# FFN operands emitted chunk by chunk, convolution columns loaded one mixer sooner, and a probability tile's two parts read bank by bank

## The chip, the cores and the metric

The kernel runs on one core of one Trainium2 chip. The metric is the device time of one execution in microseconds (us), as a median over several runs. The core has a matrix engine (PE in the profile, its weight loads PEld), a vector engine (DVE), a scalar engine (ACT), GpSimd (POOL) and the SyncE queue that starts transfers (SP, shown as SPq).

## The reference, cut to what matters

Two network blocks run one after the other on 1,024 tokens of width 1,024, all in float32. Block one has a differential attention layer and a latent attention layer (MLA, 8 heads). Block two has a mixing layer, made of a gated spatial mixer, six stick-breaking heads and six dilated-window heads, and then a feed-forward layer (FFN) with a short convolution:

```python
def _mla(...):                                   # block one, second layer
    sc = (einsum('bqhd,bkhd->bhqk', qn, k_nope) + einsum('bqhr,bkr->bhqk', qp, k_pe)) * scale
    p = softmax(sc)
    return einsum('bhqk,bkhd->bqhd', p, v)       # p times v

def second_block(...):
    h = _rmsnorm_2(x, g_mix[l]) * (1.0 + scale1) + shift1
    a_u, a_v, b_q, b_k, b_v, c_q, c_k, c_v = split(h @ w_in[l])
    y = concat([spatial_gating(a_u, a_v), stick_breaking(b_q, b_k, b_v), dilated_window(c_q, c_k, c_v)])
    x = x + (1.0 + gate1) * (y @ w_out[l])
    h = _rmsnorm_2(x, g_ffn[l]) * (1.0 + scale2) + shift2
    up = causal_dwconv(h @ w_up[l], conv_w[l], conv_b[l])
    gate, val = split(up)
    x = x + (1.0 + gate2) * ((silu(gate) * val) @ w_down[l])
```

## The kernel before, in words

Every float32 operand of a product is held as two parts that PE reads at a faster rate: an upper part `hi` (a cast, by ACT) and a lower part `lo = x - hi` (a subtraction, mostly by DVE). A product is then three matmuls, or four where one factor is exact.

The program is one long Python function. A scheduler orders each engine's instructions by priority, which is the order in which the code emits them, lifted by `ahead(tc, generator, offset)` for attention work; so a change in the order of the code can move instructions on every engine. Tiles come from pools with a fixed number of buffers per tag (`h4`, `pt`, `e`, `t2`, `wr` and so on); a load into a tag whose buffers still come from an earlier stage is preceded by a one-column copy on GpSimd (`load`).

The stretches of the profiled execution are: differential attention 0 to 800 us; MLA projections to 1045, MLA heads to 1435; in the mixing layer the gated and the dilated mixers to about 1835 and three pairs of stick-breaking heads to about 2093; then the output projection, the FFN's normalisation (`next_h`) and the FFN (a Strassen product of 7 instead of 8 block products) to the end. Next to an attention's steps the projections of the next head or pair run as filler, paced by `merge` and `pace`; beside the last pair runs the first half of the output projection.

**pt_fill.** In MLA heads and in stick-breaking heads the probabilities of 128 queries (a row block, `slot`) are turned for the product with v. PE transposes up to four 128x128 tiles into one PSUM bank (`ps`, seen in the trace as `m<-cr,e`), ACT casts them in pairs to `hi` (`pt<-m`), DVE subtracts to `lo` (`pt<-m,pt`), and `pv` then multiplies (`m<-pt,v`). The framework keeps two engines from reading one PSUM bank at the same time: they take turns, each with a wait on the other.

**mixers.** The list of six attentions is 0 to 2 dilated, 3 to 5 stick-breaking pairs 0 to 2. After the loop over the first five, `columns` loads the convolution weights (`load_rows`: three small transfers from `in_conv_w_dram` into two `t2` tiles on SP's queue) and turns them (`turn_rows`: one PE transpose and one DVE copy each).

**next_h.** For each half of the tokens, 8 chunks of 128x512 are scaled (DVE, `scalar_tensor_tensor`), shifted (ACT, `Identity` with a bias), and those of half 0 are made into FFN operands by `operand` (a cast on ACT, a subtraction on DVE, `h<-ab,h`).

Of the kernel before, what the change touches and what calls it, by code (L numbers as in the profile page):

```python
# [44 lines left out]
def alternate(a, b):  # L45

    for _ in a:
        next(b, None)
        yield
    yield from b  # L50


def drain(g):
    for _ in g:
        pass


def ahead(tc, gen, offset):

    if not offset:  # L60
        yield from gen
        return
    while True:
        with tc.high_priority(offset):
            x = next(gen, drain)
        if x is drain:
            return
        yield x


def some(g, n):

    for _ in range(n):
        if next(g, drain) is drain:
            return
        yield


def merge(main, fill, lead=0):

    for _ in range(lead):
        next(fill, None)
    for _ in main:
        next(fill, None)
    drain(fill)


def pace(main, total, early, fill, n):

    w = done = 0  # L90
    for x in main:
        w += x or 1
        if next(early, 0) == 0:
            while done < n * w / total:
                next(fill, None)
                done += 1
    drain(early)
    drain(fill)
# [24 lines left out]
class Net:  # L123
# [446 lines left out]
    def next_h(self, proj, xbox, acc, acol, shift):  # L570


        nc = self.nc
        hs, ops, phase = [], {}, self.phase
        for half in range(2):
            self.phase = phase
            drain(proj[half])
            self.phase = phase + 1
            xt, rr = xbox[half][1], self.stat_end(acc[:, half], D)
            for c in range(8):  # L580
                nc.vector.scalar_tensor_tensor(xt[c], xt[c], acol[:, c:c + 1], rr, ALU.mult, ALU.mult)
                nc.scalar.activation(xt[c], xt[c], AF.Identity, bias=shift[:, c:c + 1])
            hs.append(xt)
            if half == 0:
                for i, c in ((1, 0), (2, 4)):
                    ops[i] = [self.operand(x) for x in xt[c:c + 4]]
        return hs, ops

    def turn_ops(self, ops, b11, b12, b21, b22):
# [223 lines left out]
    def pt_fill(self, pts, p, slot, ktiles):  # L813

        nc = self.nc
        qs = slice(slot * 128, slot * 128 + 128)
        for g in range((ktiles + 3) // 4):
            n = min(4, ktiles - 4 * g)
            ps = self.pm((128, 4, 128))
            for i in range(n):  # L820
                kt = 4 * g + i
                nc.tensor.transpose(ps[:, i], p[:, kt * 128:(kt + 1) * 128], self.ident)
            for i in range(0, n, 2):
                m = min(2, n - i)
                hi, lo = (pts[4 * g + i + x][:, 0:m, qs] for x in range(2))
                nc.scalar.copy(hi, ps[:, i:i + m])
                self.lo(lo, ps[:, i:i + m], hi)

    def pv(self, v, pts):

# [1103 lines left out]
    def mixers(self, hts):  # L1934
        nc, a = self.nc, self.a
        w = a["w_in_2"][0]
        od = self.scratch([8, 128, S], "od2")
        self.od2 = od
        lse, fac = self.scratch([2, 6, S], "lse"), self.scratch([6, S], "fac")
        dil = (1, 4, 16)  # L1940

        def qk(i, box):
            return self.mixer_c_qk(w, i, dil[i], hts, box) if i < 3 else self.mixer_b_qk(w, i - 3, hts, box)

        vcol = lambda i: 2432 + i * 128 if i < 3 else 1280 + (i - 3) * 128
        self.off_b = self.mask_tile("off_b", ALU.is_gt, [[-1, 128]], 1)
        ma = self.mixer_a(w, hts, od)
        def qkv(i, box, vbox):
            yield from qk(i, box)
            yield from self.mixer_v(w, vcol(i), hts, dil[i] if i < 3 else 1, vbox)  # L1950

        box, vbox = [], []
        next(ma)
        next(ma)
        drain(alternate(qkv(0, box, vbox), some(ma, 4)))
        for i in range(5):
            cur, cv, box, vbox = box, vbox, [], []
            nxt = qkv(i + 1, box, vbox)
            if i < 3:
                att = self.mixer_c_attention(i, dil[i], *cur, cv, lse, od)  # L1960
                merge(ahead(self.tc, att, HP_C), alternate(ma, nxt) if i == 0 else nxt, LEAD_C)
            else:
                att = self.mixer_b_attention(i - 3, *cur, cv, od)
                pace(ahead(self.tc, att, HP_B), 72, iter(()), nxt, 8)
            if i == 2:
                self.alphas_c(lse, fac)
        self.columns("cols_a", 88, ["conv_w0", "conv_w1"])
        self.columns("cols_b", 56, ["conv_w2"])
        m2 = self.mod
        acol = self.scale_col(self.col["g_ffn_2"], m2["scale_f"], "acol3")  # L1970
        self.xs3 = self.scratch([D, S], "xs3")
        ots = [[None] * 8, [None] * 8]
        acc = self.t("z", [128, 2, 512])
        self.sign = acc[:, 0, 0:1]
        xbox = [[], []]
        proj = [
            self.out_proj(a["w_out_2"][0], ots[half], m2["gate_m"], self.xs2, self.xs3, half, tags, [None],
                          [acc[:, half]], xbox[half])
            for half, tags in enumerate((("kk", "kk", "ab", "ab"), ("pt",) * 4))]
        cs = ((0, 1), (2, 3), (5, 6), (7,))  # L1980
        self.last_head(
            self.mixer_b_attention(2, *box, vbox, od, ots), 20, 52, iter(()),
            [self.load_o(od, half, cs, ots[half], fac) for half in range(2)], proj[0])
        return self.next_h(proj, xbox, acc, acol, m2["shift_f"])
# [176 lines left out]
```

## Time and profile before

| | before |
|---|---|
| median of 3 runs | 2925.15 us (2916.08 to 2933.80) |
| the profiled execution | 2909.92 us, of which the span is 2907.9 us |
| PE busy, of the span | 2629.5 us, 90% |
| DVE busy | 2099.3 us, 72% |
| ACT busy | 1421.6 us, 49% |
| POOL busy | 1292.2 us, 44% |

The span runs from the first to the last recorded instruction; 2.0 us lie around it. An engine's busy time says how much of the span it worked; idle time is put down to what ended it. A wait of PE counts for most here, since PE is nearest to full.

### The profile page before, as it was taken

What the parts mean: (1) busy time and instruction counts of PE and PEld (TensorE: products, weight loads), DVE (VectorE), ACT (ScalarE), POOL (GpSimd) and SP (SyncE); (2) the same over time, 40 slices, a digit from 0 to 9 for tenths busy, and PEclk for the clock granted to TensorE, in tenths of its full rate; (3) what the DMA queues carried; (4) which work ended last, traced back from release to release, by engine and by line L of the source; (5) the groups of instructions that cost most, each with busy time, mean ns of one, the idle gap of its engine ahead of it and who ended that gap; (6) DMA issues with size and microseconds to landing.
All of it is one profiled execution on the core that took longest, in us unless ns stands there. A gap on an engine that the chain in (4) does not pass through costs nothing. (4 is left out here: it accounts for less than half of the span.)

```text
span 2907.9 us, 34523 instructions
## 1 busy us (share of the span) xinstructions
PE 2629.5 (90%) x12023; PEld 2128.7 (73%) x12023; DVE 2099.3 (72%) x2696; ACT 1421.6 (49%) x2609; POOL 1292.2 (44%) x779
## 2 busy tenths in 40 slices
PE   7899999998899979999997798887978999997897
PEld 4678787887777867877775687776766777776676
DVE  7577877778642596667768563778768888899865
ACT  5455555556444534544554453667544344443432
POOL 2423323342344532212243332444447878778761
PEclk8999999999999999999998999999989999998998
DMA  7233333234541473223342356332621222234564
GB/s 292 66 97 101 109 109 105 66 95 141 174 131 42 127 254 106 71 89 118 117 132 80 80 82 112 91 87 85 197 89 51 88 79 73 87 124 146 187 237 147
DMA packets 308402, 338.91 MB, mean 117 GB/s; under 512 B 37428, under 2 KB 232068, under 8 KB 308228
## 3 DMA queue, kind: packets, MB, share of 16 engines
q1 hardware_dynamic: 308228, 336.69, 39.3%
q8 instruction: 96, 1.57, 0.2%
q14 instruction: 78, 0.64, 0.1%
HBM read 231.17 MB, written 60.89 MB: 100 GB/s over the span
## 5 line engine op out<-in xcount | busy, mean ns | idle before, releaser
L111 PE MATMUL m<-h,wh 128*128 128x512 f32 x3480 | 985.0, 402 | 48.1 <-DVE h L111 14.4
L111 PEld LDWEIGHTS m<-h,wh 128*128 128x128 f32 x3480 | 669.4, 194 | 204.2 <-DVE h L111 18.2
L111 POOL TENSOR_TENSOR wl<-wr,wh 128x1024 fp32r<-128x1024 f32 (+1 forms) x146 | 333.5, 2291 | 429.6 <-ACT wh L111 393.4
L111 PE MATMUL u<-h,wh 128*128 128x512 f32 x1264 | 408.3, 404 | 1.4 <-ACT h L111 0.8
L111 POOL TENSOR_SCALAR e<-e,cf 128x1024 f32<-128x1024 f32 x128 | 152.6, 1193 | 564.8 <-DVE cf L111 403.5
L111 PE MATMUL m<-h,wl 128*128 128x512 f32 x840 | 336.8, 402 | 7.8 <-POOL wl L111 7.8
L111 ACT ACTIVATE e<-s,cf 128x1024 f32<-128x1024 f32 x192 | 216.0, 1126 | 240.4 <-DVE cf L111 221.9
L111 ACT CAST wh<-wr 128x1024 fp32r<-128x1024 f32 (+3 forms) x252 | 202.6, 810 | 170.1 <-PE m L111 67.7
L111 DVE TENSOR_REDUCE cf<-s 128x1 f32<-128x1024 f32 x192 | 228.3, 1217 | 69.6 <-PE s L111 69.2
L111 PEld LDWEIGHTS u<-h,wh 128*128 128x128 f32 x1264 | 233.1, 191 | 47.5 <-ACT h L111 1.2
L111 PE MATMUL u<-h,wl 128*128 128x512 f32 x632 | 252.5, 400 | 12.7 <-POOL wl L111 12.7
L111 PE MATMUL s<-kk,qq 128*128 128x512 f32 (+3 forms) x752 | 187.3, 386 | 35.8 <-DVE e L111 18.7
L111 ACT CAST pt<-m 128x256 fp32r<-128x256 f32 (+2 forms) x396 | 140.1, 376 | 155.1 <-PE m L111 88.4
L111 PE MATMUL s<-h,wh 128*128 128x512 f32 x720 | 182.8, 399 | 35.5 <-DVE h L111 18.2
L111 PEld LDWEIGHTS m<-h,wl 128*128 128x128 f32 x840 | 164.1, 195 | 44.5 <-POOL wl L111 9.0
L111 DVE SCALAR_TENSOR_TENSOR e<-z,cf,e 128x1023 f32<-128x1023 f32 (+1 forms) x88 | 175.8, 2008 | 24.8 <-ACT e L111 24.6
L111 PE MATMUL s<-h,h 128*128 128x512 f32 x640 | 171.5, 414 | 20.8 <-DVE h L111 14.3
L111 PEld LDWEIGHTS s<-h,wh 128*128 128x128 f32 x720 | 136.5, 192 | 71.3 <-DVE h L111 19.7
L111 DVE TENSOR_TENSOR pt<-m,pt 128x256 fp32r<-128x256 f32 (+2 forms) x396 | 155.0, 416 | 41.6 <-ACT pt L111 34.6
L111 PEld LDWEIGHTS s<-kk,qq 128*128 128x128 f32 x752 | 135.9, 196 | 65.8 <-DVE e L111 20.4
L111 PE MATMUL m<-pt,v 128*128 128x512 f32 (+3 forms) x668 | 151.9, 371 | 17.1 <-ACT pt L111 8.6
L111 PEld LDWEIGHTS s<-h,h 128*128 128x128 f32 x640 | 122.3, 196 | 52.5 <-DVE h L111 17.8
(285 smaller groups left out, 4848.0 us busy)
## 6 DMA issues: line engine op xcount, KB each, us to landing
wr<-in_w_in_dram SPq DMA_DIRECT2D x61, 512.0 KB
wr<-in_w_out_dram SPq DMA_DIRECT2D x48, 512.0 KB
tb<-in_w_ada_dram SPq DMA_DIRECT2D x48, 512.0 KB
wr<-in_w_up_dram SPq DMA_DIRECT2D x47, 512.0 KB
qq<-ab SPq DMA_DIRECT2D x144, 128.0 KB
wr<-in_ada_w_dram SPq DMA_DIRECT2D x32, 512.0 KB
tf<-act SPq DMA_DIRECT2D x30, 512.0 KB
wr<-in_w_down_dram SPq DMA_DIRECT2D x30, 512.0 KB
```

Of the source, the lines that this page charges most:

```text
L111: ins = f(*args, **kw)
```

## The change

Three edits. In `next_h` the operand of a chunk of half 0 is emitted straight after the chunk's scale and shift, and no longer after all eight chunks. In `pt_fill` all casts of a bank are emitted first and then all its subtractions, where before each cast was followed by its subtraction. In `mixers` the convolution weights are loaded into their two `t2` tiles ahead of stick-breaking pair 1 (`i == 4`); the transposes stay after the loop.

```diff
@@ next_h
             xt, rr = xbox[half][1], self.stat_end(acc[:, half], D)
+            for i in (1, 2):
+                ops.setdefault(i, [])
             for c in range(8):
                 nc.vector.scalar_tensor_tensor(xt[c], xt[c], acol[:, c:c + 1], rr, ALU.mult, ALU.mult)
                 nc.scalar.activation(xt[c], xt[c], AF.Identity, bias=shift[:, c:c + 1])
+                if half == 0:
+                    ops[1 + c // 4].append(self.operand(xt[c]))
             hs.append(xt)
-            if half == 0:
-                for i, c in ((1, 0), (2, 4)):
-                    ops[i] = [self.operand(x) for x in xt[c:c + 4]]
@@ pt_fill
                 nc.tensor.transpose(ps[:, i], p[:, kt * 128:(kt + 1) * 128], self.ident)
-            for i in range(0, n, 2):
-                m = min(2, n - i)
-                hi, lo = (pts[4 * g + i + x][:, 0:m, qs] for x in range(2))
-                nc.scalar.copy(hi, ps[:, i:i + m])
-                self.lo(lo, ps[:, i:i + m], hi)
+            parts = [(pts[4 * g + i], pts[4 * g + i + 1], i, min(2, n - i)) for i in range(0, n, 2)]
+            for hi, _, i, m in parts:
+                nc.scalar.copy(hi[:, 0:m, qs], ps[:, i:i + m])
+            for hi, lo, i, m in parts:
+                self.lo(lo[:, 0:m, qs], ps[:, i:i + m], hi[:, 0:m, qs])
@@ mixers, in the loop over i in range(5) and after it
             nxt = qkv(i + 1, box, vbox)
+            if i == 4:
+                rows = [self.load_rows(names) for names in (["conv_w0", "conv_w1"], ["conv_w2"])]
             ...
-        self.columns("cols_a", 88, ["conv_w0", "conv_w1"])
-        self.columns("cols_b", 56, ["conv_w2"])
+        for args, rws in zip((("cols_a", 88), ("cols_b", 56)), rows):
+            self.turn_rows(*args, *rws, self.pm((128, 128)))
```

DVE's order at the end of the first MLA head, where its last product with v goes into `t` and the next head's operand `h` is split; `pt` are subtractions of two banks (`m_9237` and `m_9246`), `z` is an accumulation of the next block's modulation:

```order
 L111 TENSOR_TENSOR t_1454_8947<-m_9185,t_1454_8947 128x512
+L111 TENSOR_TENSOR pt_9213<-m_9237,pt_9212 128x2x128
+L111 TENSOR_TENSOR pt_9215<-m_9237,pt_9214 128x2x128
 L111 SCALAR_TENSOR_TENSOR z_11384<-tb_11783,cf,z_11384 128x1024
-L111 TENSOR_TENSOR pt_9213<-m_9237,pt_9212 128x2x128
+L111 TENSOR_TENSOR pt_9217<-m_9246,pt_9216 128x2x128
+L111 TENSOR_TENSOR pt_9219<-m_9246,pt_9218 128x2x128
+L111 TENSOR_TENSOR h_1512_9267<-m_9268,h_1512_9267 128x512
 L111 SCALAR_TENSOR_TENSOR z_11384<-tb_11786,cf,z_11384 128x1024
-L111 TENSOR_TENSOR h_1512_9267<-m_9268,h_1512_9267 128x512
```

Four subtractions, a bank's two next to each other, now stand ahead of `h`, and one of the two accumulations now stands behind it.

DVE's order in stick-breaking pair 0, where its second half of the queries begins; `e` are the clamps (minima) of the scores of successive row blocks, `tb` is a scan, `t` the sum of a product with v. Before:

```order
 L111 SCALAR_TENSOR_TENSOR tb_15668<-cf,tb_15668 128x1024
 L111 TENSOR_TENSOR pt_15486<-m_15507,pt_15485 128x2x128
 L111 TENSOR_SCALAR e_15758<-s_15752 128x640
 L111 TENSOR_SCALAR e_15785<-s_15779 128x768
 L111 TENSOR_TENSOR t_2483_15194<-m_15471,t_2543_15480 64x512
 L111 TENSOR_TENSOR pt_15486<-m_15534,pt_15485 128x2x128
 L111 TENSOR_TENSOR pt_15488<-m_15507,pt_15487 128x2x128
 L111 TENSOR_TENSOR pt_15490<-m_15516,pt_15489 128x128
 L111 TENSOR_SCALAR e_15813<-s_15807 128x896
```

And of the change, the same place:

```order
 L111 TENSOR_TENSOR t_2483_15194<-m_15471,t_2543_15480 64x512
 L111 TENSOR_SCALAR e_15758<-s_15752 128x640
 L111 TENSOR_TENSOR pt_15486<-m_15507,pt_15485 128x2x128
 L111 TENSOR_TENSOR pt_15488<-m_15507,pt_15487 128x2x128
 L111 TENSOR_TENSOR pt_15490<-m_15516,pt_15489 128x128
 L111 TENSOR_TENSOR pt_15486<-m_15534,pt_15485 128x2x128
 L111 TENSOR_TENSOR pt_15488<-m_15534,pt_15487 128x2x128
 L111 TENSOR_SCALAR e_15785<-s_15779 128x768
 L111 SCALAR_TENSOR_TENSOR tb_15668<-cf,tb_15668 128x1024
 L111 TENSOR_SCALAR e_15813<-s_15807 128x896
```

The second clamp now stands behind five subtractions in a row, and the scan behind the first two clamps.

SP's queue, where the convolution weights are started; `wr` is a block of output weights, `od` an attention result that is written to memory. Before, at the end of pair 1:

```order
 L111 DMA wr_17198<-in_w_out_dram 128x8x128
-L111 DMA t_2755_16588<-in_conv_w_dram 44x128 x2
-L111 DMA t_2757_16595<-in_conv_w_dram 44x128
-L111 DMA od_13122<-t_2680_16181 128x512
```

And of the change, at the end of pair 0:

```order
 L111 DMA wr_16942<-in_w_out_dram 128x8x128
+L111 DMA t_2619_15891<-in_conv_w_dram 44x128 x2
+L111 DMA t_2620_15895<-in_conv_w_dram 44x128
 L111 DMA od_13122<-t_2544_15484 128x512
```

The three transfers are started one pair of heads sooner, again just ahead of the write of an attention result.

## Rows read from the trace of the kernel before

**Rows 1.** The page: span, and busy time, share of the span and number of instructions of each engine.

```profile
span 2907.9 us, 34523 instructions
PE 2629.5 (90%) x12023; PEld 2128.7 (73%) x12023; DVE 2099.3 (72%) x2696; ACT 1421.6 (49%) x2609; POOL 1292.2 (44%) x779
```

**Rows 2.** Busy time by stretch (MLA heads, stick-breaking pairs): us of the stretch, then busy us and number of instructions of PE, PEld, DVE, ACT and POOL, the granted clock as a share of full speed, the share of the DMA engines and GB/s.

```profile
1045.00:1435.00 390.00, 365.91 (x1843) 301.00 (x1842) 273.13 (x546) 193.53 (x450) 95.64 (x85) 0.97 0.37 114
1835.00:2093.00 258.00, 216.44 (x1061) 178.82 (x1062) 205.66 (x284) 164.87 (x328) 117.98 (x63) 0.93 0.36 102
```

**Rows 3.** The instructions on tile `pt`, MLA heads: engine, operation, count, shortest, median and longest in ns, first and last start, forms.

```profile
L111 ACT CAST pt<-m x234: 361/373/422, 1050.0 to 1431.0; 128x256 fp32r<-128x256 f32 x117
L111 DVE TENSOR_TENSOR pt<-m,pt x233: 398/416/426, 1055.0 to 1434.7; 128x256 fp32r<-128x256 f32 x117
```

**Rows 4.** Waits of all engines, MLA heads: who waited, for whom, us in total, times, longest.

```profile
ACT pt L111 <- DVE pt L111: 47.2, 55, 2.4
DVE pt L111 <- ACT pt L111: 22.6, 32, 3.0
```

**Rows 5.** Waits of PE alone, 1045 to 1400 us, same columns.

```profile
PE s L111 <- DVE h L111: 8.5, 3, 3.5
PE m L111 <- DVE pt L111: 1.3, 2, 0.8
```

**Rows 6.** Busy time in stretches of 10 us behind the start of three MLA heads, columns as in rows 2.

```profile
1140.00:1150.00 10.00, 10.00 (x48) 8.15 (x47) 8.21 (x16) 4.21 (x12) 0.73 (x1) 0.83 0.59 200
1240.00:1250.00 10.00, 9.37 (x38) 7.60 (x39) 7.23 (x15) 3.87 (x12) 0.73 (x1) 0.69 0.71 240
1340.00:1350.00 10.00, 7.43 (x26) 6.00 (x26) 8.18 (x13) 2.86 (x9) 0.43 (x1) 0.66 0.39 135
```

**Rows 7.** The timelines of DVE, ACT and PE around the start of an MLA head (1131 to 1142 us), and of PE at two later heads: start, us, engine, operation, tiles, count, and in brackets the idle time before it and what ended it.

```profile
1134.82 0.68 DVE L111 TENSOR_TENSOR t<-m,t 128x512 f32<-128x512 f32 x1
1135.49 1.28 DVE L111 SCALAR_TENSOR_TENSOR z<-tb,cf,z 128x1024 f32<-128x1024 f32 x1
1136.70 0.42 DVE L111 TENSOR_TENSOR pt<-m,pt 128x256 fp32r<-128x256 f32 x1
...
1138.54 0.69 DVE L111 TENSOR_TENSOR h<-m,h 128x512 fp32r<-128x512 f32 x1
...
1132.51 0.37 ACT L111 CAST pt<-m 128x256 fp32r<-128x256 f32 x1 [5.55 <-PE m L111]
...
1137.15 0.65 ACT L111 CAST pt<-m 128x256 fp32r<-128x256 f32 x2 [0.46 <-DVE pt L111]
...
1139.28 1.19 PE L111 MATMUL s<-h,h 128*128 128x512 f32 x4 [2.53 <-DVE h L111]
...
1240.63 2.08 PE L111 MATMUL s<-h,h 128*128 128x512 f32 x4 [2.54 <-DVE h L111]
...
1342.57 2.07 PE L111 MATMUL s<-h,h 128*128 128x512 f32 x4 [3.45 <-DVE h L111]
```

**Rows 8.** Waits of PE, stick-breaking pairs (1830 to 2093 us), columns as in rows 4.

```profile
PE s L111 <- DVE e L111: 18.7, 13, 6.4
PE m L111 <- DVE pt L111: 4.5, 6, 1.6
PE m L111 <- DMA t<-in_conv_w_dram: 2.2, 2, 2.1
PE m L111 <- ACT pt L111: 0.8, 2, 0.5
```

**Rows 9.** Waits of ACT and DVE for each other at `pt`, stick-breaking pairs (1835 to 2093 us), columns as in rows 4.

```profile
ACT pt L111 <- DVE pt L111: 7.1, 6, 2.1
DVE pt L111 <- ACT pt L111: 5.8, 10, 1.4
```

**Rows 10.** The timelines of DVE and of PE where the second half of stick-breaking pair 0 begins (1876 to 1888 us), columns as in rows 7.

```profile
1878.54 2.47 DVE L111 TENSOR_TENSOR_SCAN tb<-cf,tb 128x1024 f32<-128x1024 f32 x1 [0.26 <-ACT tb L111]
1880.93 0.39 DVE L111 TENSOR_TENSOR pt<-m,pt 128x256 fp32r<-128x256 f32 x1
1881.24 1.67 DVE L111 TENSOR_SCALAR e<-s 128x640 f32<-128x640 f32 x2
...
1883.67 0.95 DVE L111 TENSOR_TENSOR pt<-m,pt 128x256 fp32r<-128x256 f32 x3
...
1882.11 1.86 PE L111 MATMUL s<-kk,qq 128*128 128x512 f32 x4 [3.05 <-DVE e L111]
```

**Rows 11.** The timelines of PE, SP and POOL at the turning of the convolution weights (1999 to 2007 us), columns as in rows 7.

```profile
2005.41 0.27 PE L111 MATMUL m<-cr,t 88*128 88x88 f32 x1 [2.06 <-DMA t<-in_conv_w_dram]
...
2003.44 1.11 SPq L111 DMA_DIRECT2D t<-in_conv_w_dram  x3
...
2003.23 0.30 POOL L111 COPY t<-z 128x1 f32<-128x1 f32 x2
```

**Rows 12.** The last subtraction of an FFN operand of half 0 on DVE, and PE at the start of the FFN (2118 to 2152 us), columns as in rows 7.

```profile
2122.73 0.68 DVE L111 TENSOR_TENSOR h<-ab,h 128x512 fp32r<-128x512 f32 x1
...
2151.59 0.63 PE L111 MATMUL m<-h,wh 128*128 128x512 f32 x1
```

**Rows 13.** Groups of DVE instructions, stick-breaking pairs: count, busy us, mean ns of one, idle time before.

```profile
L111 DVE TENSOR_TENSOR h<-tf,h 128x512 fp32r<-128x512 f32 x14 | 12.9, 956 | 0.8 <-ACT h L111 0.7
L111 DVE TENSOR_TENSOR z<-z,tf 128x512 f32<-128x512 f32 x7 | 12.3, 1760 | 1.0 <-ACT tf L111 0.7
```

## The prediction

> **What bounds the kernel now.** I read the page first: PE is busy 2629.5 of 2907.9 us, DVE 72%, and nothing else is above half [rows 1]. PE sets the end, so an edit is worth what it takes out of PE's waits, stage by stage. Next the busy time by stretch. In the MLA heads PE works 365.91 of 390 us, so 24.1 us is all that any edit could win there without making matmuls faster; in the stick-breaking pairs it works 216.44 of 258 us (41.6 us idle) with DVE at 205.66 us, so there the two engines share the limit [rows 2]. Then PE's waits in these two stretches, since they name what the changed code could have delayed. In the MLA heads the largest is three waits of 8.5 us together, where a head's first scores wait for DVE's split of `h`; DVE's `pt` subtractions are named for 1.3 us only [rows 5]. In the stick-breaking pairs PE waits 18.7 us for the clamps `e`, 4.5 and 0.8 us for the two parts of `pt`, and 2.2 us for the convolution weights [rows 8].
>
> What the reader should notice is the difference between two lists: ACT and DVE wait for each other at `pt` for 47.2 + 22.6 us in the MLA heads [rows 4] and 7.1 + 5.8 us in the stick-breaking pairs [rows 9], but PE waits for `pt` for 1.3 us and 5.3 us. The larger list is idle time of engines that are not full there (ACT works 193.53 of 390 us [rows 2]); it costs only where PE stands behind it.
>
> The profiled execution took 2909.92 us, 15.2 us (0.5%) under the median of 2925.15. The sum below is made on the former and carried to the median as a difference.
>
> **pt_fill in the MLA heads.** Nothing is added or removed: 256 casts and 256 subtractions (8 heads x 8 row blocks x 4) of 373 and 416 ns [rows 3]. Before, a bank went ACT, DVE, ACT, DVE, three handoffs; now it is ACT, ACT, DVE, DVE, one. A handoff can be seen: ACT's cast at 1137.15 starts when DVE's subtraction, begun at 1136.70 and 0.42 us long, is over [rows 7]. With 128 banks and the 69.8 us of mutual waiting [rows 4] that is about 0.55 us a bank, nearly all beside PE's filler matmuls.
>
> Where it reaches PE is the start of a head. I redid the first such place with the new order, with the durations of [rows 7]. `t` ends at 1135.5. Two subtractions follow, 0.75 us (0.42 for one, less its overlap with the next), to 1136.25; their casts were free to run from 1132.51 on. One accumulation `z`, 1.2 us from start to next start, to 1137.45; two more subtractions to 1138.2; then `h`, 0.69 less overlap, done at 1138.85. In the trace `h` starts at 1138.54 and ends at 1139.2, and PE's scores start at 1139.28. So they start some 0.33 us sooner: two accumulations (2.4 us) and one subtraction ahead of `h` became one accumulation and four subtractions. Three places of this kind give 1.0 us. Elsewhere PE is full (10.00 of 10 us behind this very place [rows 6]). I take **-1.5 us**, the 1.0 and some of the 1.3 us for `pt`. The bounds: nothing; and the 8.5 us gone wholly together with the slow clock behind them. The three stretches of 10 us after these waits have granted clocks of 0.83, 0.69 and 0.66 [rows 6], so they lack 1.7 + 3.1 + 3.4 = 8.2 us of full-speed work: -16.7 us. I stay near the lower end, since `h` still stands behind a bank's worth of DVE work.
>
> **pt_fill in the stick-breaking pairs.** 120 subtractions here, in 72 banks, of which 48 hold two pairs and change their order; the rest keep it. What PE loses to `pt` is 4.5 + 0.8 = 5.3 us [rows 8]: the product with v needs the last bank's `lo`, which came after a handoff. A handoff saved is worth about a cast, 0.37 us, and there were six plus two waits, of 0.66 us in the mean; I take two thirds, **-3.5 us**. The bounds: nothing, and 5.3 + 5.8 = -11.1 us, if DVE's own waits for ACT [rows 9] go as well and all of it reaches PE, DVE being near full.
>
> The order also changes around the clamps, for which PE waits 18.7 us. At the start of the second half of pair 0 the scan (2.47 us) now stands behind the first two clamps, but the second clamp stands behind five subtractions. Redone with [rows 10]: the first clamp is over at about 1880.8 instead of 1882.06, the second at 1883.5 instead of 1882.9. The first releases PE's scores at 1882.11, the second the next; one is 1.3 us sooner, one 0.6 us later. I take 0 for this, and keep the loss as a rival.
>
> **The convolution weights.** Before, the three transfers were started at 2003.44, and PE, at their transposes, waited 2.06 us at a stretch [rows 11], 2.2 us in all [rows 8]. Started a pair sooner they have landed long before: **-2.2 us**, with nothing else of PE's in that gap. What moves with them: two GpSimd copies of one column, 0.30 us together, and three starts on SP, 1.11 us [rows 11]. They now hold two `t2` tiles through pair 1, so a result tile `y` could wait for a buffer, and on SP the write of pair 0's result and the weight blocks are queued behind the starts, which wait for POOL's copies. A write of a result is needed only by the output projection, a pair later. I put 0 on this, and 2 us at most: the 2.2 us wait of before, met again elsewhere.
>
> **The FFN operands.** The row order of ACT and of DVE at this place is the same before and after, only tile numbers differ: the scheduler already mixed scale, shift and split chunk by chunk. And the last split ends at 2123.4 while PE takes up the first FFN product at 2151.59 [rows 12], behind the second half of the output projection, 28 us of cover. **0 us**; without that cover a late operand would cost at most its own 0.68 us per chunk.
>
> **Sum.** -1.5 - 3.5 - 2.2 = -7.2, rounded to -7: 2903 for the profiled execution, 2918 on the median, 0.25% down.
>
> **Rivals.** *Nothing but the weights.* PE's filler covers every handoff, as 365.91 of 390 us and the 1.3 us for `pt` suggest; the order only swaps which DVE work is late. Then -2.2, with 2 either way: 2923.
>
> *The gaps close.* For it speaks that each of the three large waits is followed by slow clock [rows 6]: four scores take 2.08 and 2.07 us at the two later heads and 1.19 us at the first [rows 7]. If the shorter handoffs remove the waits and the slow stretches: -16.7 - 11.1 - 2.2 = -30: 2895. Against it: my redone place gives a tenth of it.
>
> *Slower.* A bank's subtractions in one block are a longer unit of DVE work ahead of a clamp. Five at 0.32 us (three in a series take 0.95 us [rows 10]) are 1.6 us; at the six second halves that is 9.6 us, and where the wait grows past what the filler covers, a slow stretch of 3.4 us follows [rows 6], at three of them 10.2. With the -2.2: +18, 2943. It decides if the second clamp, not the first, is what PE's next scores wait for, with no projection matmuls left to fill. Against it: the same move brings the first clamp 1.3 us sooner.
>
> *Collisions on DVE.* Seven additions `z<-z,tf` take 1.76 us and fourteen splits `h<-tf,h` 0.956 us in the mean, where an operation of that size takes 0.68 us elsewhere [rows 12, 13]; something stretches them. If the new order puts the fourteen splits where the additions are, they take 1.76 us: 14 x 0.80 = +11.3 us, and with the -7.2, +4: 2929. The Trainium skill, page "SBUF — State Buffer", section "Who interferes with whom", has a rule for this: GpSimd and DVE share one pair of ports, locked by whichever instruction starts first, and a DVE operation with two inputs in SBUF needs it. By that rule the moved subtractions (one input in PSUM) are not stretched themselves, and they agree, 398 to 426 ns over the whole MLA stretch [rows 3]; the splits and additions next to them could be.
>
> **How the numbers follow.** The likeliest, a gain of 1 to 12 us, holds 0.50, centred on -7; nothing but the weights 0.17; gaps closing 0.20, of which little more than half goes beyond 14.6 us; slower through the clamps 0.09; collisions 0.04. A measurement of this kernel can tell about 0.5% (14.6 us) from no change, the spread of its three runs being 0.6%. Faster by more than that: the better part of the gaps closing, a tail of the likeliest, and the runs of before lying high by their own spread, 0.26. Slower by more: 0.12. Same: 0.62. The range reaches from -30 to +15, the slower rival short of its full price: 2895 to 2940.
>
> **What would show it.** Right: the conv row vanishes from PE's waits; mutual waits at `pt` fall by at least half in both stretches; PE's wait for `pt` in the pairs falls to 2 us; the three starts of MLA heads keep waits near 2 us for `h`; FFN from 2185 us on takes the same time. The gaps rival would show as granted clock of 0.9 or more in the three stretches after the head starts. The slower one as more than 25 us of PE's waits for `e`. The prediction is wrong if the MLA or the pairs' stretch differs by more than 12 us, or if any stretch before 1045 us moves at all.

## The result

The changed kernel takes 2890.13 us in the median of 4 runs (2884.81 to 2894.17), the kernel before 2920.61 us beside it; the ratio is 0.9894, with a 95% interval of 0.9861 to 0.9927: 1.1% faster, 21 to 41 us. My 2918 was 28 us too high, and the low end of the range, 2895, was 5 us too high as well.

The page of the changed kernel:

```profile
span 2887.1 us, 34666 instructions
PE 2617.6 (91%) x12023; PEld 2121.7 (73%) x12023; DVE 2089.5 (72%) x2696; ACT 1414.4 (49%) x2609; POOL 1304.3 (45%) x779
```

The same number of instructions on each of these engines (the total also holds instructions that this line does not count), a span 20.8 us shorter, and PE busy 11.9 us less [rows 1]: a share of the gain is PE doing the same matmuls in less time.

The place is one. The two traces run level up to the first MLA head (the scores of its third row block start at 1042.8 us before, 1042.4 now) and again from the mixing layer on: there the changed kernel is ahead by 19 to 23 us up to the end, at nearly every matmul outside the stick-breaking pairs. So I take the MLA heads between two fixed instructions, from those scores to the first projection matmul of the mixing layer, here and in all that follows. Busy time of before: the whole stretch, then four pieces of it; columns as in [rows 2] (us, PE, PEld, DVE, ACT and POOL busy, granted clock, DMA):

```profile
1042.80:1444.60 401.80, 377.71 (x1888) 310.38 (x1887) 283.21 (x567) 197.20 (x460) 97.14 (x86) 0.97 0.38 119
1140.40:1143.80 3.40, 3.40 (x12) 2.82 (x11) 3.40 (x6) 0.97 (x3) 0.00 (x0) 0.50 0.80 272
1239.40:1246.20 6.80, 5.57 (x15) 4.50 (x16) 5.98 (x11) 1.55 (x5) 0.00 (x0) 0.50 0.82 288
1341.80:1348.60 6.80, 6.03 (x16) 4.86 (x17) 6.38 (x11) 1.02 (x3) 0.00 (x0) 0.50 0.40 147
1433.90:1440.70 6.80, 5.90 (x18) 4.67 (x19) 5.98 (x17) 3.35 (x9) 2.23 (x2) 0.50 1.00 339
```

And of the changed kernel, the stretch and its last 333.6 us:

```profile
1042.40:1422.60 380.20, 369.54 (x1887) 303.75 (x1886) 270.33 (x563) 192.09 (x461) 101.76 (x86) 0.99 0.41 125
1089.00:1422.60 333.60, 328.74 (x1699) 271.12 (x1698) 229.90 (x494) 170.22 (x410) 85.40 (x75) 1.00 0.36 109
```

The stretch went from 401.8 to 380.2 us, -21.6. PE's idle time in it (the stretch less PE busy) went from 24.1 to 10.7 us, -13.4. PE's busy time went from 377.7 to 369.5, -8.2, for the same matmuls: before, PE ran at half speed (granted 0.50, 1.2 of 2.4 GHz) for 3.4, 6.8, 6.8 and 6.8 us at the waits at three head starts and at the end, from 1.1 us behind the first wait and from within the other three; in the changed kernel the clock is 1.00 from 1089 us on. Ahead of that it has half speed twice, for 3.4 us from 1054.9 us (the kernel before has the same from 1055.0) and for 3.4 us from 1085.6, behind a wait of 1.71 us.

PE's waits in that stretch, 1045 to 1415 us, of the changed kernel (who waits for whom, us, times, longest):

```profile
PE m L111 <- DVE pt L111: 4.9, 4, 1.7
PE s L111 <- ACT e L111: 4.0, 2, 2.3
PE m L111 <- DVE t L111: 0.5, 1, 0.5
```

The waits for `h`, 8.5 us [rows 5], are gone; the one for `pt` has grown from 1.3 to 4.9. Of ACT's and DVE's waits at `pt` (all engines, 1045 to 1415 us):

```profile
ACT pt L111 <- PE m L111: 89.4, 43, 5.6
DVE pt L111 <- ACT pt L111: 20.6, 20, 2.6
```

ACT's wait for DVE (47.2 us [rows 4]) is no longer among them; its wait for PE has grown from 62.8 to 89.4. DVE's wait for ACT has hardly changed (22.6 us [rows 4]).

### PE's own order at the head starts

The order on DVE, on which my sum rested, was only half of what changed at a head start. PE's order there, before and in the changed kernel; `s` are scores, `m<-cr,e` transposes, `m_9313<-qq` the six projection matmuls of the second half of the same head's keys:

```
before
 L111 MATMUL m_9294<-cr,e_9290 128x128 x4
 L111 MATMUL s_9429<-h_1512_9267,h_1482_9105 128x512
 L111 MATMUL s_9492<-h_1512_9267,h_1482_9105 128x512
 L111 MATMUL s_9429<-h_1512_9267,h_1482_9105 128x512 x2
...
 L111 MATMUL m_9303<-cr,e_9290 128x128 x4
...
 L111 MATMUL m_9313<-qq_7838,wh_9261 128x512
changed
 L111 MATMUL m_9294<-cr,e_9290 128x128 x4
 L111 MATMUL m_9303<-cr,e_9290 128x128 x4
 L111 MATMUL s_9429<-h_1512_9267,h_1482_9105 128x512
 L111 MATMUL s_9492<-h_1512_9267,h_1482_9105 128x512
 L111 MATMUL m_9313<-qq_7838,wh_9261 128x512
...
 L111 MATMUL m_9313<-qq_7843,wl_9262 128x512
 L111 MATMUL s_9429<-h_1512_9267,h_1482_9105 128x512 x2
```

In the third row of scores PE needs the part of `h` that DVE makes. Before, it stood there, with the second bank's transposes and the projections behind it. Now both are ahead of it. The same place in the trace of the changed kernel (timelines of PE and of DVE, 1130 to 1145 us; columns as in [rows 7]):

```profile
1130.73 0.71 PE L111 MATMUL m<-cr,e 128*128 128x128 f32 x5
...
1134.17 0.73 PE L111 MATMUL s<-h,h 128*128 128x512 f32 x2
1136.08 0.70 PE L111 MATMUL m<-qq,wh 128*128 128x512 f32 x2 [1.18 <-DVE pt L111]
...
1137.55 1.09 PE L111 MATMUL s<-h,h 128*128 128x512 f32 x4
...
1130.92 1.28 DVE L111 SCALAR_TENSOR_TENSOR z<-tb,cf,z 128x1024 f32<-128x1024 f32 x1 [0.44 <-DMA tb<-in_w_ada_dram]
1132.12 0.68 DVE L111 TENSOR_TENSOR t<-m,t 128x512 f32<-128x512 f32 x1
1132.72 0.75 DVE L111 TENSOR_TENSOR pt<-m,pt 128x256 fp32r<-128x256 f32 x2
1133.99 1.28 DVE L111 SCALAR_TENSOR_TENSOR z<-tb,cf,z 128x1024 f32<-128x1024 f32 x1 [0.52 <-DMA tb<-in_w_ada_dram]
...
1135.85 0.68 DVE L111 TENSOR_TENSOR h<-m,h 128x512 fp32r<-128x512 f32 x1
```

PE still waits 1.18 us, for the subtraction that frees the projections' bank, then works through them while DVE splits `h`, and the scores follow with no wait. Before, PE had waited at this head ahead of the transposes too (timeline of PE, 1134 to 1141 us):

```profile
1135.65 0.63 PE L111 MATMUL m<-cr,e 128*128 128x128 f32 x4 [1.39 <-DVE t L111]
```

These 1.39 us and the 2.53 us for `h` [rows 7] became 1.18 us, and no half-speed clock follows.

DVE's side moved too, and not as my sum had it. From the start of `t` to the end of `h` DVE takes 4.41 us in both traces (1134.82 to 1139.23 [rows 7], 1132.12 to 1136.53 above): one accumulation fewer lies between them, but the one that is left waits 0.52 us for its transfer. What came sooner is `t`. Ahead of it DVE stands until a block of modulation weights (`tb<-in_w_ada_dram`) has landed, 0.44 us now and 1.53 us before (timelines of PE and DVE of before, 1131 to 1142 us):

```profile
1131.82 0.71 PE L111 MATMUL m<-cr,e 128*128 128x128 f32 x5
...
1133.62 1.28 DVE L111 SCALAR_TENSOR_TENSOR z<-tb,cf,z 128x1024 f32<-128x1024 f32 x1 [1.53 <-DMA tb<-in_w_ada_dram]
```

PE reached these transposes 1.1 us sooner (1131.82, now 1130.73) and `h` was done 2.7 us sooner, so `h` is 1.6 us closer behind PE. Read in the same way at all three head starts, from the start of the product with v ahead of them, `h` is done after 12.95, 13.2 and 12.8 us before and after 11.3, 11.1 and 11.8 us now, and DVE's waits for these transfers on the way are 1.8, 1.9 and 2.9 us before, 1.0, 0.8 and 1.5 us now. No run moved the transfers alone, so why they come sooner is not shown.

### The profile page after: what moved, and what is told of

The parts are those of the page before. It is cut to its first block, busy times and chain, and to the rows that moved or that the text cites. A ratio compares the mean times of both kernels' runs of the same rounds, so it can differ in the third digit from the quotient of the medians.

```text
span 2887.1 us, 34666 instructions
## 1 busy us (share of the span) xinstructions
PE 2617.6 (91%) x12023; PEld 2121.7 (73%) x12023; DVE 2089.5 (72%) x2696; ACT 1414.4 (49%) x2609; POOL 1304.3 (45%) x779
## 5 line engine op out<-in xcount | busy, mean ns | idle before, releaser
L111 PE MATMUL m<-h,wh 128*128 128x512 f32 x3480 | 983.0, 402 | 46.7 <-DVE h L111 12.9
L111 PE MATMUL s<-h,wh 128*128 128x512 f32 x720 | 184.5, 402 | 36.9 <-DVE h L111 18.2
L111 PE MATMUL s<-kk,qq 128*128 128x512 f32 (+3 forms) x752 | 185.7, 384 | 32.5 <-DVE e L111 15.5
L111 ACT CAST pt<-m 128x256 fp32r<-128x256 f32 (+2 forms) x396 | 126.0, 387 | 114.3 <-PE m L111 109.2
L111 PE MATMUL s<-h,h 128*128 128x512 f32 x640 | 167.7, 408 | 11.5 <-DVE h L111 5.8
L111 DVE TENSOR_TENSOR pt<-m,pt 128x256 fp32r<-128x256 f32 (+2 forms) x396 | 146.4, 415 | 36.0 <-ACT pt L111 34.9
L111 PE MATMUL m<-pt,v 128*128 128x512 f32 (+3 forms) x668 | 148.8, 368 | 22.2 <-ACT pt L111 11.9
L111 DVE TENSOR_TENSOR pt<-t,pt 128x256 fp32r<-128x256 f32 x256 | 95.8, 416 | 85.6 <-ACT pt L111 79.4
```

Source lines behind the costliest of these rows:

```text
L111: ins = f(*args, **kw)
```

## The experiments

Times are ratios to the kernel before, run beside each, with 95% intervals; "the MLA stretch" is the one bounded above (401.8 us before; the expectations of the first two groups quote the cruder 390 of [rows 2]).

**Which edit.** Four kernels, each with a part of the change alone.

e1, `pt_fill` alone, as in the change, nothing else:

> The bank-wise reading in pt_fill alone, in MLA heads and stick-breaking pairs; next_h and the convolution weights as before. Theory M (everything comes from pt_fill in the MLA heads, where the shorter use of a PSUM bank lets projection matmuls stand ahead of the scores that wait for h): 20 to 30 us under the kernel before, ratio 0.990 to 0.993, the stretch of the MLA heads some 370 us instead of 390, a granted clock of 0.98 or 0.99 there. Rival S (the gain is spread, each edit has a share): 10 to 15 us under, and the MLA stretch 378 or more.

Measured: 2890.47 us, ratio 0.9899 (0.9874 to 0.9924), MLA stretch 377.1.

e2, all but `pt_fill`. No run took `next_h` alone, but the trace of e2 has the order of before on ACT and on DVE everywhere except from 1965 to 2071 us, in the stick-breaking pairs; at `next_h` it is the same. So this is the convolution weights' move, together with the reordering in the pairs that it brings:

> next_h and the convolution weights changed, pt_fill as before. Theory M: 0 to 3 us under the kernel before, ratio 0.999 to 1.000; the MLA stretch at 390 us with its waits for h of about 8.5 us and half-speed clock behind them at the same places; the wait for the convolution weights gone. Rival S: 8 us or more under. My sum on record gave these two edits -2.2 us together.

Measured: 2915.51 us, ratio 0.9981 (0.9966 to 0.9997). The MLA stretch and one of the half-speed pieces, as before (busy time, columns as above):

```profile
1040.00:1441.70 401.70, 377.51 (x1888) 310.12 (x1887) 282.97 (x567) 197.00 (x460) 97.07 (x86) 0.97 0.39 119
1236.40:1243.20 6.80, 5.28 (x14) 4.22 (x15) 6.28 (x11) 1.84 (x6) 0.00 (x0) 0.50 0.89 319
```

The wait for the weights is no longer among PE's. -5.6 us, with an interval of -10 to -1 that holds my -2.2.

e3, bank-wise in the MLA heads alone, and e4, in the stick-breaking pairs alone:

```diff
-    def pt_fill(self, pts, p, slot, ktiles):
+    def pt_fill(self, pts, p, slot, ktiles, bankwise):
...
+            if bankwise:
+                parts = [(pts[4 * g + i], pts[4 * g + i + 1], i, min(2, n - i)) for i in range(0, n, 2)]
...
+            else:
+                for i in range(0, n, 2):
...
-                self.pt_fill(pts, e, slot, 8)
+                self.pt_fill(pts, e, slot, 8, True)
...
-                self.pt_fill(pts, u, slot, qi + 1)
+                self.pt_fill(pts, u, slot, qi + 1, False)
```

The two branches are the order of the change and that of before. The calls are those of e3; e4 has them the other way round, False in the MLA heads and True in the pairs, and e5 and e6 below have `half == 1` and `half == 0` in the MLA heads and False in the pairs.

> Bank-wise reading in the MLA heads alone, hi, lo, hi, lo as before in the stick-breaking pairs, nothing else changed. Theory M: the same time as the whole change within 4 us (ratio 0.990 to 0.993), the MLA stretch 370 us. Rival S: half of it. My sum on record gave this part -1.5 us.

> Bank-wise reading in the stick-breaking pairs alone, nothing else changed. Theory M: within 3 us of the kernel before, ratio 0.999 to 1.001. Rival S, and my sum on record: 3.5 us under or more, with PE's waits for pt in the pairs down from 5.3 us to about 2.

Measured: e3 2893.31 us, 0.9909 (0.9884 to 0.9934), MLA stretch 380.0; e4 2921.25 us, 1.0001 (0.9983 to 1.0019). So the gain is `pt_fill` in the MLA heads, and in the stick-breaking pairs it is worth nothing that can be measured: the interval is -5 to +6 us, which does not exclude my -3.5, but PE's waits for `pt` there are 8.1 and 2.4 us and not about 2. Rival S fell. The MLA stretch of e4, whose order there is that of before, is 398.7 us, against 401.8 and 401.7 (e2); two of its half-speed pieces last 3.4 us instead of 6.8. So the stretch of one trace is good to some 3 us.

**The order at the head starts, or each bank's share.** e5 and e6 read half of the MLA banks bank-wise; only e5's order puts the six projection matmuls ahead of the scores as the change does.

> Bank-wise reading in the MLA heads for the second half of the queries alone (64 of 128 banks), the rest as before. In the instruction order this alone puts the six projection matmuls of the next head ahead of the scores that wait for h. Theory F (what counts is PE's work in that hole, not the number of handoffs): nearly the whole gain, 15 to 28 us under the kernel before, no half-speed clock behind the four head starts. Rival H (each bank read in one go saves its share): half of the gain, 10 to 14 us under.

> Bank-wise reading in the MLA heads for the first half of the queries alone (the other 64 banks). Eight or ten scores still stand ahead of the six projection matmuls at the head starts. Theory F: 0 to 6 us under the kernel before; waits for h and the half-speed clock remain at these places. Rival H: half of the gain, 10 to 14 us under.

Measured: e5 2910.43 us, 0.9964 (0.9945 to 0.9984); e6 2903.0 us, 0.9938 (0.9916 to 0.9961). The MLA stretch of e5:

```profile
1044.80:1435.90 391.10, 370.27 (x1887) 304.88 (x1887) 280.00 (x565) 195.05 (x461) 97.43 (x86) 0.99 0.40 122
```

The MLA stretch of e6:

```profile
1044.50:1433.60 389.10, 370.93 (x1887) 305.01 (x1886) 275.56 (x566) 195.25 (x461) 102.22 (x86) 0.99 0.40 121
```

And PE's largest waits in e6 there (1040 to 1425 us):

```profile
PE s L111 <- ACT e L111: 4.6, 4, 2.3
PE s L111 <- DVE h L111: 3.7, 3, 2.6
```

-10.7 and -12.7 us: each half of the banks has about half of the gain, and they add up to 23.4 where the whole has 21.6. My theory F, that the projections' place in the order is everything, fell: e6 gains without it, with the wait for `h` down from 8.5 to 3.7 us (2.6 of them at another place, 1086.7 us), and e5, which has it, gains no more. The traces show two ways to the same end. In e5 `h` is done no sooner, 13.5, 13.6 and 13.3 us behind the start of the product with v, but the projections fill PE's time and no wait for `h` is left. In e6 the projections stand behind the scores, but `h` is done after 11.5, 10.3 and 11.7 us. The change has both. In e5 and e6 most of the slow clock is gone already (PE busy 370.3 and 370.9 us, 377.7 before and 369.5 with the change), while of the idle time 20.8 and 18.2 us are left (24.1 before, 10.7 with the change).

e7 and e8 keep the handoffs as they are (e7 those of before, e8 those of the change) and emit the filler one step earlier:

```diff
-            merge(ahead(self.tc, self.mla_attention(...), HP_M), fill)
+            merge(ahead(self.tc, self.mla_attention(...), HP_M), fill, 1)
```

> pt_fill, next_h and the convolution weights as before; the MLA filler (v's projection and the next head's operands) is only emitted one step earlier against the attention's row blocks. All three handoffs a bank remain. Theory F: the waits for h at the head starts go and the MLA stretch is 10 us or more shorter, 375 to 380 us instead of 390. Rival H: the waits move elsewhere, the stretch stays at 385 us or more.

> The whole change, and the MLA filler emitted one step earlier as well. Theory F: there is no hole left to fill, so within 5 us of the change alone (ratio to the kernel before 0.988 to 0.992). Rival H: the two gains add up, 5 us or more below the change.

Measured: e7 2919.74 us, 0.9993 (0.9977 to 1.0009); e8 2893.46 us, 0.9902 (0.9875 to 0.9929). In e7 PE waits elsewhere for the same DVE work; its MLA stretch (of the slowest of its 12 runs, and with twelve matmuls fewer, which now stand ahead of it):

```profile
1050.30:1449.30 399.00, 375.21 (x1876) 307.69 (x1877) 276.70 (x562) 197.63 (x456) 104.63 (x86) 0.97 0.38 116
```

And the largest of PE's waits in it (1040 to 1425 us):

```profile
PE m L111 <- DVE h L111: 10.4, 4, 3.4
```

Moving the filler without shortening the handoffs does nothing that can be measured. Moving it on top of the change does nothing either, as theory F had it, so no hole is left there for it.

**ACT and DVE waiting for each other, or a bank held too long.** e9 gives each pair of tiles a bank of its own, in the MLA heads alone, and otherwise leaves hi, lo, hi, lo:

```diff
-        for g in range((ktiles + 3) // 4):
-            n = min(4, ktiles - 4 * g)
+        for g in range((ktiles + per - 1) // per):       # per = 2 in the MLA heads, 4 elsewhere
+            n = min(per, ktiles - per * g)
```

> pt_fill as before, hi, lo, hi, lo, but in the MLA heads each pair of transposed tiles has a PSUM bank of its own, so ACT and DVE never wait for each other over one bank more than once a pair; twice as many of the four shared banks are asked for. Theory W (the harm of before is that ACT and DVE wait for each other, which makes DVE late with h, t and v): ACT's waits for DVE at pt fall to near nothing and 15 to 25 us are gained, the MLA stretch 377 to 387 instead of 401.8 (measured from the first head's scores to the first matmul of the mixing layer's projections). Rival K (the harm is that a bank is held too long, so that PE's transposes and projections find none free): no gain or a loss, 398 us or more, since banks are now scarcer.

Measured: 2930.19 us, ratio 1.0039 (1.0022 to 1.0055), slower. Its waits in the MLA stretch (of all engines at `pt`, 1045 to 1435 us, and of PE alone to 1445):

```profile
ACT pt L111 <- PE m L111: 127.7, 60, 6.9
DVE pt L111 <- ACT pt L111: 39.6, 18, 5.0
...
PE m L111 <- DVE pt L111: 11.3, 10, 1.7
...
PE s L111 <- DVE h L111: 3.1, 3, 1.5
...
PE m L111 <- DVE t L111: 0.4, 1, 0.4
```

And its MLA stretch:

```profile
1042.80:1455.70 412.90, 382.43 (x1888) 306.42 (x1886) 273.61 (x564) 194.28 (x459) 100.75 (x86) 0.98 0.38 114
```

ACT's waits for DVE are gone here as in the change, and the stretch is 11 us longer: PE is busy 4.7 us longer and idle 6.4 us more. PE finds no free bank among the four that transposes, projections and products with v share: its wait for `pt` is 11.3 us, 1.3 before, and eight of the ten waits are of transposes. But its wait for `h` fell here as well, from 8.5 to 3.1 us, and that for `t` from 3.1 to 0.4. So e9 shows that scarcer banks cost more than the vanished mutual waits bring; it does not decide against theory W, that DVE's lateness was the harm. That PE's delay before the change came from banks held by `pt` is not shown: there PE's only two waits for `pt` are of products with v, and no run held a bank longer and changed nothing else.

**Is the half-speed clock a consequence of the wait?** e10 and e11 add useless work to the kernel before, at the place of the wait:

```diff
+                    if h in (2, 4, 6) and half == 0 and slot < 2 and kh == 0:
+                        for _ in range(4):                # e11: 6
+                            nc.tensor.matmul(o, q[:, 0, ql], k[:, 0], start=True, stop=True)
                     nc.tensor.matmul(o, q[:, 0, ql], k[:, 0], start=True, stop=False)
```

> The kernel before with useless work: at the start of heads 2, 4 and 6 the first score matmul of two row blocks is repeated four times (24 matmuls, 5.5 us at 0.227 each), at the place where PE waits for h; start flags make the repeats leave no trace in the result. Theory C (the half-speed clock follows PE's idling, and the idling is what the change took away): the half-speed stretches behind these starts (17 us in the trace of before) vanish or halve and the MLA stretch gets shorter than 401.8, by 3 to 8 us, although work was added. Rival: the clock falls there anyway or the wait stays, so 402 us or more, half-speed as before.

> The same with six repeats (36 matmuls, 8.2 us), which cover the whole of the waits for h of 2.53, 2.54 and 3.45 us. Theory C: the half-speed stretches behind the three starts vanish, the MLA stretch 393 to 399 us. Rival: 403 us or more.

Measured: e10 2907.39 us, 0.9963 (0.9948 to 0.9978); e11 2907.96 us, 0.9963 (0.9947 to 0.9979), MLA stretch 395.4. Kernels that do more are 0.37% faster. Of e10 the MLA stretch, and 369 us of it:

```profile
1044.30:1439.40 395.10, 377.34 (x1911) 309.10 (x1910) 283.02 (x567) 197.36 (x461) 97.52 (x86) 0.99 0.40 120
1059.70:1428.40 368.70, 356.44 (x1829) 292.77 (x1828) 260.80 (x527) 187.14 (x437) 90.03 (x81) 1.00 0.37 109
```

PE in e10 at the first of the three starts (timeline, 1134 to 1146 us):

```profile
1137.44 2.55 PE L111 MATMUL s<-h,h 128*128 128x512 f32 x10
1140.32 1.19 PE L111 MATMUL s<-h,h 128*128 128x512 f32 x4 [0.33 <-DVE h L111]
```

The wait of 2.53 us is 0.33, the clock stays at 1.00 over all three starts, and the stretch is 6.7 us shorter than that of before (3.6 than that of e4) with PE busy 377.3 us as before, although 5.5 us of matmuls were added. At the fourth place, the wait for `v` of 3.4 us that e10 does not fill, the clock falls as before (granted 0.50 from 1428.4 to 1435.2 us). So at the three starts the clock fell because PE stood, and with 8.2 of 21.6 us it is a sizeable share of what the change took away. The Trainium skill, page "TensorE: Matmul & The Clock Gate", section "HAM oscillation — how this bites in real kernels", describes it for waits on transfers: such a wait between bursts of matmuls brings the clock down, and the next burst starts slow. The rows agree, granted 0.50 at each of the four waits of before, at none of the three that e10 fills, and at the fourth still.

**A version from it.** e12 is the change plus 16 useless matmuls of 256 columns ahead of each sum of squares (`stat_sum`):

> The whole change, and useless matmuls (16 of 256 columns, 1.8 us) ahead of each sum of squares that ends a normalisation from the end of the latent attention on, ten places; their bank is overwritten by the sum that follows. In the trace of the change PE waits 4.58, 4.28 and 2.94 us at three of these, with half-speed stretches of 6.8, 3.4 and 3.4 us behind. Theory C (half-speed clock follows PE's idling): those stretches shrink, and the time is 2 to 7 us below the change, some 2884 to 2889, ratio to the kernel before 0.986 to 0.990. Rival: the clock stays as it is there, and the work where nothing is waited for costs 2 to 6 us over the change.

Measured: 2887.83 us, 0.989 (0.9866 to 0.9913): under the change by 2.3 us, which the intervals do not separate. At the first of the three waits it is some 4 us quicker, and the half-speed piece there is gone; in the profiled execution a wait for a transfer later on (4.0 us, 0.4 in the change; see what stays open, below) took that back, and the mean granted clock of the two profiled executions is the same, 0.958. Inconclusive.

## Why the prediction was wrong, step by step

**pt_fill in the MLA heads: -1.5 predicted, -21.6 measured.** This is the step that failed: the sum kept the three waits for `h`, less 0.33 us each, and put nothing on the clock behind them. In the runs these waits are gone, PE's idle time in the stretch fell by 13.4 us and its busy time by 8.2. It failed in three ways.

First, I redid the head start with DVE's new order, took the time of `t` as given and left PE's order as it was. My result, `h` 0.33 us sooner, came out 1.0 to 2.1 us. At the head that I redid nothing of it lies behind `t`, where I had looked; at all three DVE waited 0.8 to 1.4 us less for the modulation's transfers, which none of my rows held. And PE's order had changed at the same place, so that PE had the projections to do while `h` was made. e6 has the former without the latter and e5 the latter without the former, and each has about half of the gain. From 4 to 6 us were won at each of the three head starts, and as much at the end of the stretch.

Second, "PE is full (10.00 of 10 us behind this very place [rows 6])" was misread. That row has a granted clock of 0.83: PE was busy there because it ran the same matmuls at half speed for 3.4 us. A busy share at a reduced clock is no cover; it is part of the cost of the wait ahead of it.

Third, even my bound of -16.7 fell short. It took the three waits for `h` and their slow clock, left out those for `t` and `cf`, and I had cut the list of waits at 1400 us, ahead of the one for `v` (PE of before, 1045 to 1435 us):

```profile
PE m L111 <- DVE v L111: 3.4, 1, 3.4
PE m L111 <- DVE t L111: 3.1, 2, 1.7
PE m L111 <- DVE cf L111: 2.4, 3, 1.2
```

The wait for `v` stands at the end of the stretch, and 6.8 us at half speed begin in it. In the changed kernel (PE, 1042.4 to 1422.6 us) 0.4 us is left for `v`, 0.5 for `t` and nothing for `cf`. The 24.1 us of idle time that I gave as "all that any edit could win there without making matmuls faster" was the right ceiling for waits, 13.4 of it came, and the clock's 8.2 came on top.

**Stick-breaking pairs: -3.5 predicted, nothing measured** (e4, 1.0001, -5 to +6 us). Of ACT's and DVE's waits for each other at `pt`, 12.9 us [rows 9], this is left in the changed kernel (all engines, 1815 to 2072 us):

```profile
DVE pt L111 <- ACT pt L111: 4.1, 5, 1.3
```

That is as forecast. But PE's own waits (PE alone, 1810 to 2073 us) moved on:

```profile
PE s L111 <- DVE e L111: 15.5, 12, 6.5
PE m L111 <- DVE pt L111: 8.5, 8, 6.1
PE m L111 <- ACT tf L111: 8.4, 4, 5.2
PE m L111 <- DVE t L111: 7.8, 2, 7.1
```

3.2 us less for the clamps and 4 more for `pt` than in [rows 8], and 7.8 for `t`, which had 1.3: DVE works 80% of this stretch [rows 2]; that an order there only chooses whom it serves late is my reading, and no run tests it. My sign of rightness, "PE's wait for `pt` falls to 2 us", failed.

**Convolution weights: -2.2 predicted, -5.6 measured** (e2), with the interval down to -1; right in kind, though it also holds what the reordered pairs give or take, and the size cannot be told from mine. **FFN operands: 0**, and the order of the instructions is the same; no run took them alone.

**The rivals.** *The gaps close* (0.20) named the right mechanism, the waits at head starts together with the slow clock behind them, and its 2895 is the nearest of all. That it came so near is in part luck, since its split was not right: it needed 11.1 us from the pairs, which gave nothing, and only 16.7 from the MLA heads. My reason against it was the redone place. *Slower* did not come: PE's waits for the clamps fell, 18.7 to 15.5. *Collisions on DVE* partly did. In the pairs, DVE's groups of the changed kernel:

```profile
L111 DVE TENSOR_TENSOR h<-tf,h 128x512 fp32r<-128x512 f32 x14 | 20.2, 1464 | 1.5 <-ACT h L111 1.4
L111 DVE TENSOR_TENSOR z<-z,tf 128x512 f32<-128x512 f32 x7 | 9.4, 1346 | 0.8 <-ACT tf L111 0.8
```

The fourteen splits take 20.2 us instead of 12.9, the seven additions 9.4 instead of 12.3 [rows 13], 4.4 us more of DVE in all, while the stretch itself (257 us, 258 before) did not get longer. What stretches them can be read from the timelines of DVE and POOL: of these 42 operations in the two traces 20 took 0.85 to 2.88 us, each with a GpSimd operation (`wl<-wr,wh` or `e<-e,tb`) beside it from its start, and the other 22 took 0.66 to 0.69. That agrees with the rule that the prediction takes from the Trainium skill, page "SBUF — State Buffer", section "Who interferes with whom".

Right were: the mutual waits falling by more than half, the end of the weights' wait, the FFN unmoved (723.1 us against 722.9), hardly a matmul before 1045 us moved by more than some 1 us. Wrong was that the three starts keep waits near 2 us for `h`; the sign of the gaps rival, a granted clock of 0.9 or more behind them, came with 1.00. The mark "wrong if the MLA stretch differs by more than 12 us" was met.

**What stays open.** The two traces differ by 20.8 us, the medians by 30. The interval (21 to 41) begins about at the former. The profiled execution of before lies 11 us under its kernel's median, that of the changed one 1.3. One wait that varies from one execution to the next is seen in the dilated mixer, where PE waits for a transfer: 0.4 us in both traces, but of e4, for one:

```profile
1793.55 0.66 PE L111 MATMUL s<-kk,qq 128*128 128x128 f32 x2 [6.70 <-DMA qq<-pt]
```

It was over 2.7 us in six of the thirteen profiles of before, of the change and of e1 to e11 (e2 and e4 to e8), among them e8, which has the whole change. Whether the change makes it rarer is not settled, and with it some 9 us of the 30.

## What to carry to other kernels

Where two engines read one PSUM bank in turn, try letting each do all its reads in one go: it adds no instruction and saves two handoffs a bank. It paid in the MLA heads (21.6 us) and not measurably in the pairs; giving each pair of tiles a bank of its own saved handoffs as well and cost 0.4%. When a change lets a scheduler move instructions, redo the critical place with the new order of every engine that waits there, above all of PE, not only of the engine that was edited, and with the transfers that they wait for. A wait of PE is to be priced with the half-speed stretch behind it, and a busy PE at a reduced granted clock is a loss, not a cover.

## What the runs showed of the hardware that I had not expected

Useless matmuls in a wait made a kernel faster: 24 of them, 5.5 us of work, gave a ratio of 0.9963 (0.9948 to 0.9978), since three half-speed stretches of 3.4, 6.8 and 6.8 us did not come. In the kernel before, each of the waits of 2.53, 2.54 and 3.45 us for `h` was met by granted 0.50, from 1.1 us behind its end at the first and from within it at the other two, and these places came back in another kernel with the same order within a few us (e2: 1137.4, 1236.4, 1338.8 and 1431.0 us, 3.4 us long and three times 6.8).
